# Order of the pairs in the first block of a merged projection stage: four plain pairs instead of three ahead of the first one with seven products

## The chip, the cores and the metric

One core of one Trainium2 chip runs the kernel. The metric is the device time of one execution in microseconds (us); less is better. The engines of the core are TensorE (PE, matrix multiplies), VectorE (DVE), ScalarE (ACT), GpSimd (POOL) and SyncE (SP, which here only issues loads). They run side by side and wait for one another through semaphores.

## The reference

A decoder layer of 256 positions and 2048 channels in float32. Latent attention and a gated short convolution run on the same normalised input. Each is projected back to 2048 channels, and the two are merged by gates that are projections of the input:

```python
proj = jnp.einsum('bsd,de->bse', h, w_in)          # ... z_mla, c_in, b_gate, c_gate, z_conv, g_mla, g_conv
...
y_mla = jnp.einsum('bse,ed->bsd', attn, w_o_mla)
...
y_conv = jnp.einsum('bse,ed->bsd', b_gate * conv * jax.nn.silu(z_conv), w_o_conv)
merged = jax.nn.sigmoid(g_mla) * y_mla + jax.nn.sigmoid(g_conv) * y_conv
out = jnp.einsum('bsd,de->bse', merged, w_out)
x = x + _rmsnorm(out, post_norm_g)
```

The merged stage, of which this document tells, computes the four projections of the line `merged = ...`: the two gates and the two outputs y_mla and y_conv, each 256 x 2048 by 2048 x 2048.

## The kernel before

**Precision.** Every float32 operand is split into a high part (a copy on ACT that rounds it, `whi`, `th`, `mix` hi) and a low part (the rest, a subtraction on DVE, `wlo`, `tl`, `mix` lo); `split_act` (L281) does both. A product (L264) is three matmuls: high by high, high by low, low by high. All matmuls are recorded at L90 and keep the order of the program on PE (L88).

**Weights.** All weights come in units of up to 128 x 2048 values (1 MB). `plan` lists them in the order of their use. `ahead` (L237) loads a unit into one of three `raw` tiles, up to three units ahead (SP issues the loads, in this order, L173), and splits the unit after the one that is now taken (`split_unit`, L180). A plain unit is split in two halves of 1024 columns, each into a `whi` and a `wlo` tile; there are five tiles of each, used in turn (L212, L213). So a high half is written only when PE is done with the half that held its tile before.

**The merged stage** has four projections n (0 and 1 the gates, 2 and 3 the outputs), and each has two blocks c of 1024 output columns. A block sums over eight pairs of 128 input channels. One unit of weights is one pair: four quarters of 512 columns (two channel groups by two column groups), and the two halves t of the 256 positions make a 2 x 2 by 2 x 2 block product. A plain pair takes its eight products (24 matmuls), into the banks p2, q3, q4 and d22. For the pairs in `fast` the kernel uses a scheme of seven products (21 matmuls, L1033 to L1039) instead, in the order p1, q5, q7, q6, p2, q3, q4, into seven banks. This is done in projections 0 and 1: pairs 0, 3 and 5 (`FAST`), except in the very first block, (0, 0), where only pairs 0 and 3 are (L144).

**What a pair with seven products needs.** On the side of the weights, `split_seven` (L218) makes three sums on DVE (`ts`, L224: one of 1024 columns and two of 512) and splits them too (`th` and `tl`; the names t1 to t4 are their quarters; two tiles of each). On the side of the input, `mixed(k)` (L1004) makes on DVE one sum (`xr`, L1008) and four differences (`xm`, L1012) of the input's blocks, and splits the result into `mix`. This is kept for all four blocks that use it, so `mixed` runs only in block (0, 0): `between` calls it for pair 0 at the block's place 1, for pair 3 at place 3 and for pair 5 at place 5 (L1106). `xr` and `xm` share two tiles (`ev`). These tiles lie where the stage before had its own, and can be written only when that stage's last steps on DVE are done.

**What comes after the seven products.** `first_sums` (L1052: one copy on ACT, L1053, and four sums on DVE) joins the banks p1, q5, q6 and q7 into the gate tiles. It is called at the place after the last pair with seven products (L1068). `last_sums` (L1059) adds p2, q3, q4 and d22 when the block is over, and a sigmoid follows on ACT (L1115). PSUM has eight banks, and a block uses all of them, so the next block may write a bank only when these sums have read it.

**What sets the order.** The matmuls keep program order, as do some helpers (`tc.keep_in_program_order`). The order of the other instructions on DVE and ACT is set when the kernel is built, by a planner that simulates the program and takes at each point the ready instruction that comes first in program order. On the chip each engine runs its list in that order.

The change touches `pair_order[0, 0]` (L142), which the plan of the loads (L148), and `fast_block` (L1025) follow.

Of the kernel before, what the change touches and what calls it, by code (L numbers as in the profile page):

```python
# [84 lines left out]
def tile_layer(ctx: ExitStack, tc: tile.TileContext, xw, w0, xb, x, pos, pvec, post_g, wc, wz, wcv, wkr, wqk, wqr, wv, cwr, wd, wo, out):  # L85
# [53 lines left out]
            u_head[i][j] = add(wcv[i, j])  # L139

    pair_order = {(n, c): list(range(PAIRS)) for n in range(4) for c in range(2)}
    pair_order[0, 0] = [1, 2, 4, 0, 6, 3, 5, 7]  # L142
    fast = {(n, c): FAST if n < 2 else () for n in range(4) for c in range(2)}
    fast[0, 0] = FAST[:2]  # L144
    u_d, seven = {}, set()
# [1201 lines left out]
```

## Time and profile before

| | |
|---|---|
| median of 3 runs | 1035.17 us |
| the three runs | 1033.79, 1035.17, 1035.41 us |
| the profiled execution | 1034.48 us |
| its span, first to last instruction | 1032.7 us |
| busy: PE, DVE, ACT, POOL | 1022.6, 747.4, 543.9, 179.0 us |
| mean granted clock of TensorE | 0.997 |
| the merged stage's first block, (0, 0) | 590.23 to 639.00 us of the span |

A row of the timeline has the start in us from the span's start, the duration, engine, line of the kernel, operation, output and inputs by the names of their tiles, the number of like instructions that were merged into the row, and in brackets the idle time of the engine before it with what ended that. Several banks show under a short name: p1 and p2 as `p`, q3 to q7 as `q`, d22 as `d`. A row of the waits says who waited for whom. Where the trace knows no releaser, it says "issue". A matmul starts 0.227 us after the one before it when nothing holds it, and its own 0.39 us overlaps the next.

### The profile page before, as it was taken

Reading aid. Unit: us, or ns where it says so; the run is one execution under the profiler, and the core shown is the slowest. Engines: PE = TensorE matmul, PEld = TensorE weight load, DVE = VectorE, ACT = ScalarE, POOL = GpSimd, SP = SyncE. Lnnn points to the kernel's source line nnn. Section 1 sums busy time; section 2 is a strip of 40 time slices with the busy share of each in tenths; the row PEclk is TensorE's granted clock in tenths of the full one; section 3 lists DMA queues with packets and bytes.
Section 4 is the critical chain, followed back from the end, with each engine's and each line's share of the span. In section 5 each row is a group of like instructions: output and inputs, shape, how many; then the busy total and the mean of one; then the engine's idle time right before and its main releaser. Section 6 shows DMA issues by size and latency. Waiting matters only on the chain.

```text
span 1032.7 us, 12827 instructions
## 1 busy us (share of the span) xinstructions
PE 1022.6 (99%) x4651; PEld 851.5 (82%) x4651; DVE 747.4 (72%) x1062; ACT 543.9 (53%) x764; POOL 179.0 (17%) x344
## 2 busy tenths in 40 slices
PE   9999999999999999999999989999999999999998
PEld 7888888888888888888888868888888888888886
DVE  7588777787777777777877798898875554756572
ACT  7665545655456454564555546555654443344451
POOL 4540421104301223112133120000000000214000
PEclk9999999999999999999999989999999999999999
DMA  9775866568665676757676755555555555577852
GB/s 357 276 260 202 279 205 234 213 201 282 218 246 197 220 263 211 273 192 244 229 269 222 260 183 178 226 206 204 204 198 182 193 202 196 197 258 246 344 184 81
DMA packets 44528, 233.26 MB, mean 226 GB/s; under 512 B 7953, under 2 KB 10513, under 8 KB 21553
## 3 DMA queue, kind: packets, MB, share of 16 engines
q1 hardware_dynamic: 32400, 199.67, 54.8%
q0 software_dynamic: 11632, 29.48, 8.8%
q10 hardware_dynamic: 432, 3.29, 0.8%
q8 instruction: 36, 0.59, 0.2%
q14 instruction: 28, 0.22, 0.1%
HBM read 215.66 MB, written 12.58 MB: 221 GB/s over the span
## 4 chain that ended last, share of the span: by engine, by line
PE 97%; DVE 2%; DMA 0%; ACT 0%; issue 0%
PE cv L90 34%; PE sq L90 17%; PE q L90 8%; PE z L90 8%; PE out L90 8%; PE p L90 4%; PE d L90 2%; PE kn L90 2%; PE qa L90 2%; PE qn L90 2%; PE vv L90 2%; PE ckv L90 2%; PE sc L90 1%; PE qr L90 1%; PE o L90 1%; DVE wlo L283 1%
## 5 line engine op out<-in xcount | busy, mean ns | idle before, releaser
L283 DVE TENSOR_TENSOR wlo<-raw,whi 128x1024 fp32r<-128x1024 f32 (+1 forms) x370 | 431.8, 1179 | 202.8 <-ACT whi L282 195.4
L282 ACT ACTIVATE whi<-raw 128x1024 fp32r<-128x1024 f32 (+1 forms) x372 | 373.2, 1021 | 376.0 <-PE cv L90 116.9
L90 PE MATMUL cv<-whi,x_both 128*128 128x512 f32 x1024 | 319.8, 389 | 0.0
L90 PEld LDWEIGHTS cv<-whi,x_both 128*128 128x128 f32 x1024 | 192.3, 188 | 39.4
L90 PE MATMUL cv<-wlo,x_both 128*128 128x512 f32 x512 | 199.6, 390 | 0.0
L90 PE MATMUL sq<-whi,x_both 128*128 128x512 f32 x384 | 118.8, 389 | 0.0
L90 PEld LDWEIGHTS cv<-wlo,x_both 128*128 128x128 f32 x512 | 96.1, 188 | 19.5 <-DVE wlo L283 0.2
L90 PEld LDWEIGHTS sq<-whi,x_both 128*128 128x128 f32 x384 | 72.1, 188 | 15.0
L90 PE MATMUL z<-whi,x_both 128*128 128x512 f32 x256 | 80.0, 389 | 0.0
L90 PE MATMUL out<-whi,x_both 128*128 128x512 f32 x256 | 79.0, 389 | 0.0
L90 PE MATMUL sq<-wlo,x_both 128*128 128x512 f32 x192 | 74.7, 389 | 0.0
L367 POOL DMA_DIRECT2D far<-g x32 | 17.4, 551 | 322.5 <-DVE g L1138 289.9
L367 POOL DMA_DIRECT2D far<-via x64 | 35.2, 556 | 179.2 <-DVE via L359 178.9
L90 PEld LDWEIGHTS out<-whi,x_both 128*128 128x128 f32 x256 | 48.1, 188 | 9.9
L90 PEld LDWEIGHTS z<-whi,x_both 128*128 128x128 f32 x256 | 48.1, 188 | 9.9
L90 PE MATMUL q<-whi,x_both 128*128 128x512 f32 x168 | 55.1, 389 | 0.0
L90 PE MATMUL z<-wlo,x_both 128*128 128x512 f32 x128 | 49.8, 389 | 0.0
L90 PE MATMUL out<-wlo,x_both 128*128 128x512 f32 x128 | 49.8, 389 | 0.0
L90 PE MATMUL p<-whi,x_both 128*128 128x512 f32 x128 | 46.6, 391 | 0.0
L90 PEld LDWEIGHTS sq<-wlo,x_both 128*128 128x128 f32 x192 | 36.0, 188 | 7.4
L367 POOL DMA_DIRECT2D far<-cw x48 | 26.1, 551 | 79.1 <-DVE cw L359 79.1
L90 PE MATMUL sq<-whi,cv_first 128*128 128x512 f32 x128 | 39.7, 389 | 0.0
(253 smaller groups left out, 1433.0 us busy)
## 6 DMA issues: line engine op xcount, KB each, us to landing
raw<-wcv_dram SPq DMA_DIRECT2D x64, 1024.0 KB, 5.9
raw<-wd_dram SPq DMA_DIRECT2D x64, 1024.0 KB, 4.8
raw<-wz_dram SPq DMA_DIRECT2D x16, 1024.0 KB, 4.8
raw<-wo_dram SPq DMA_DIRECT2D x16, 1024.0 KB, 5.0
raw<-wqk_dram SPq DMA_DIRECT2D x8, 1024.0 KB, 6.1
cw<-cwr_dram POOLq DMA_DIRECT2D x24, 256.0 KB, 6.2
raw<-wc_dram SPq DMA_DIRECT2D x4, 1024.0 KB, 10.4
raw<-wv_dram SPq DMA_DIRECT2D x4, 1024.0 KB, 4.8
```

The costliest lines, as they stand in the source:

```text
L90: return tc.keep_in_program_order(nc.tensor.matmul(*a, **kw))
L282: a = nc.scalar.activation(hi, src, AF.Copy)
L283: b = nc.vector.tensor_tensor(lo, src, hi.bitcast(F32), op=ALU.subtract)
L367: tc.keep_in_program_order(queue.dma_start(out=f[i], in_=m))
```

## The change

One line. In block (0, 0) pair 6 is taken before pair 0 instead of after it, and pair 5 before pair 3. Pairs 0 and 3 are the ones with seven products. The places at which `mixed` is called stay as they are. `first_sums` follows the last pair with seven products, so it moves from place 6 to place 7, with one plain pair (7) behind it instead of two (5 and 7).

```diff
     pair_order = {(n, c): list(range(PAIRS)) for n in range(4) for c in range(2)}
-    pair_order[0, 0] = [1, 2, 4, 0, 6, 3, 5, 7]
+    pair_order[0, 0] = [1, 2, 4, 6, 0, 5, 3, 7]
     fast = {(n, c): FAST if n < 2 else () for n in range(4) for c in range(2)}
     fast[0, 0] = FAST[:2]
```

The loads, the splits and the products of these units follow the new order, since all three go by the plan. The matmuls, sums and splits are the same in number and size, and every bank sums the same terms, in another order.

## The prediction

> **What bounds the kernel now.** I read the waits of TensorE (PE) first, over the whole execution: who was waited for, the us in total, how often, and the longest.
>
> ```profile
> PE q L90 <- issue: 2.3, 1, 2.3
> PE q L90 <- DVE mix L283: 1.4, 1, 1.4
> PE idle L90 <- PEq L1335: 0.8, 1, 0.8
> PE qa L90 <- ACT whi L282: 0.5, 1, 0.5
> PE fin L90 <- ACT dg L1223: 0.4, 1, 0.4
> ```
>
> PE is the bound, and it waits five times in all. The last three are the program's head and tail. The first two have "q" as their output, the products of the merged stage, and they belong together. The timeline of PE shows where (start, duration, line, operation, idle before it and what ended that):
>
> ```profile
> 606.59 0.39 PE L90 MATMUL p<-whi,x_both 128*128 128x512 f32 x1
> 606.82 0.39 PE L90 MATMUL p<-wlo,x_both 128*128 128x512 f32 x1
> 607.04 0.39 PE L90 MATMUL p<-whi,x_both 128*128 128x512 f32 x1
> 609.74 0.77 PE L90 MATMUL q<-th,mix 128*128 128x512 f32 x1 [2.31 <-issue]
> 610.30 0.63 PE L90 MATMUL q<-tl,mix 128*128 128x512 f32 x1
> 612.31 1.22 PE L90 MATMUL q<-th,mix 128*128 128x512 f32 x2 [1.38 <-DVE mix L283]
> ```
>
> This is pair 0, the first pair with seven products: p1 (three matmuls), then q5, the first product with a mixed operand. It stands still at once, and again two matmuls later. How long should it take? The view by stretch gives its length, the busy us of PE, its weight loads, VectorE (DVE), ScalarE (ACT) and GpSimd, the granted clock, the DMA share and GB/s. First pair 0, then the plain pair 6 and the seven-product pair 3 behind it, cut at each pair's first matmul:
>
> ```profile
> 606.59:617.92 11.33, 7.64 (x23) 5.34 (x21) 10.78 (x18) 5.75 (x8) 0.00 (x0) 0.70 0.56 208
> 617.92:623.36 5.44, 5.44 (x26) 4.50 (x24) 3.90 (x7) 2.65 (x4) 0.00 (x0) 1.00 0.55 193
> 623.36:628.12 4.76, 4.76 (x23) 3.94 (x21) 4.76 (x6) 4.18 (x6) 0.00 (x0) 1.00 0.30 79
> ```
>
> Undisturbed, a plain pair takes 5.44 us (24 matmuls, 0.227 each) and a seven-product pair 4.76 (21). Pair 0 took 11.33: **6.57 us lost**. The idle time explains 3.69 of it (2.31 + 1.38); the other 2.88 is the clock, which is 0.70 in this stretch. In stretches of 5 us, from 605:
>
> ```profile
> 605.00:610.00 5.00, 2.69 (x12) 1.98 (x11) 5.00 (x7) 3.47 (x4) 0.25 (x1) 0.95 0.79 265
> 610.00:615.00 5.00, 3.62 (x8) 2.37 (x8) 4.93 (x10) 0.53 (x1) 0.00 (x0) 0.50 0.62 259
> 615.00:620.00 5.00, 5.00 (x21) 4.04 (x20) 4.52 (x10) 3.69 (x5) 0.00 (x0) 0.87 0.13 16
> ```
>
> Read as half speed, a mean of 0.95 is 0.5 us slow in the first stretch, all of the second is, and 1.3 us of the third: the clock fell near 609.5, some 2.1 us after PE fell idle (607.04 + 0.23 + a little), and came back near 616.3. So here a wait of about 2 us costs its length and then 2.9 us more; a shorter one, as an estimate from these rows, its length alone.
>
> The Trainium skill ("TensorE: Matmul & The Clock Gate", What's actually happening) puts the fall to half speed after an idle window of about 3.4 us. The trace disagrees, since a single gap of 2.31 us was followed by it; by that page of the skill the two waits would have cost 3.69 us alone, and removing them would give 1034.71 - 3.69 = 1031.0. It gets no chance of its own below, as the 6.57 us are measured.
>
> The same rows tell what PE waited for: DVE is busy 5.00 of 5.00 and 4.93 of 5.00, ACT far less. The timelines of DVE and of ACT:
>
> ```profile
> 599.83 0.66 DVE L1008 TENSOR_TENSOR xr<-x_both 128x512 f32<-128x512 f32 x1
> ...
> 606.42 1.23 DVE L224 TENSOR_TENSOR ts<-raw 128x1024 f32<-128x1024 f32 x1
> 607.55 1.23 DVE L283 TENSOR_TENSOR wlo<-raw,whi 128x1024 fp32r<-128x1024 f32 x1
> 608.69 0.69 DVE L1008 TENSOR_TENSOR xr<-x_both 128x512 f32<-128x512 f32 x1
> 609.29 1.23 DVE L283 TENSOR_TENSOR wlo<-raw,whi 128x1024 fp32r<-128x1024 f32 x1
> 610.42 1.23 DVE L283 TENSOR_TENSOR tl<-ts,th 128x1024 fp32r<-128x1024 f32 x1
> 611.56 0.69 DVE L283 TENSOR_TENSOR mix<-xm,mix 128x512 fp32r<-128x512 f32 x1
> 612.16 0.69 DVE L224 TENSOR_TENSOR ts<-ts,raw 128x512 f32<-128x512 f32 x1
> ```
>
> ```profile
> 606.17 2.00 ACT L282 ACTIVATE whi<-raw 128x1024 fp32r<-128x1024 f32 x2 [2.81 <-PE d L90]
> 608.08 1.04 ACT L282 ACTIVATE th<-ts 128x1024 fp32r<-128x1024 f32 x1
> 609.03 0.61 ACT L282 ACTIVATE mix<-xm 128x512 fp32r<-128x512 f32 x1
> ```
>
> mixed(0) begins at 599.83 and its low part ends at 612.25, with DVE never idle between. The "issue" of 2.31 us ends when ACT's mix ends (609.03 + 0.61 = 609.64), the 1.38 us when DVE's mix ends. Nothing was slow: 12.4 us of DVE work stood between the start and the end of pair 0's preparation, and only 7.4 us of PE work. Counting the halves of each unit (ring of five tiles per high and low part, so each high half waits until a former pair gives its tile back) the rows of DVE belong to: pair 3's sum (606.42), pair 6's second half (607.55), mixed(3) (608.69), pair 3's first half (609.29), pair 0's t2/t4 (610.42), its mix (611.56).
>
> **The change part by part.** No instruction is added or removed: the same weights, matmuls, splits and sums. Pair 6 changes places with pair 0, and pair 5 with pair 3; four things move.
>
> *PE's arrival.* Pair 6 now takes 606.59 to 612.03, and pair 0 starts then. q5 needs the high mix and t1 at 612.03 + 3 x 0.227 = 612.71, and the low mix, its third matmul, at 613.16.
>
> *The mix's readiness.* DVE's start at 599.83 does not move: the pairs before it are the same. Between there and 612.25 pair 6's two halves stand as before, one of them earlier in place of pair 0's first half: a swap at no cost. Pair 3's sum and first half (1.13 each, start to start) give way to the first half of pair 5, which is plain and has no sums: minus 1.13, so the low mix ends near 611.1. At the other end, the schedule might still put pair 3's three sums in front (1.13 + 0.6 + 0.6, the latter the spacing of rows as wide): 613.4. The two ends are 2.0 us before the need and 0.3 after it; I take the first, because mixed(0) and pair 0's split come before pair 3's in program order. Pair 5's second half can't get ahead cheaply: its tile comes free when PE is done with pair 6, near 611.6. If DVE were to wait for it, with 1.0 of ACT, 1.13 of DVE and the mix's 0.69, the mix would end near 614.5, 1.3 us late. The high mix ends near 609.6 as now, 3 us early.
>
> So the stall's 6.57 us go, or all but 0.3 to 1.3 of them.
>
> *What is late next: pairs 5, 3 and 7.* They start at 616.79, 622.23 and 626.99. For pair 3, t1/t3 may be written only after q7 of pair 0 has read theirs (near 614.2), t2/t4 after its q4 (616.8). By the DVE and ACT rows (1.04 and 1.13 each) they are ready near 616 and 620, where 622.9 and 624.3 is needed: no cost, some 4 us of cover. SP's queue issues the loads in the new order of units, three tiles deep; pair 0's comes one place later and pair 6's one sooner. Size and median us from issue to landing:
>
> ```profile
> raw<-wd_dram SPq DMA_DIRECT2D x64, 1024.0 KB, 4.8
> ```
>
> A load takes 4.8 us and a plain unit 5.44 of PE, with three tiles ahead: nothing.
>
> *first_sums, one unit later.* It now runs with one plain pair behind the last seven-product pair instead of two. That is the new risk, as block (0,1) opens with a seven-product pair that needs the same banks at once. In the trace:
>
> ```profile
> 623.34 1.23 DVE L224 TENSOR_TENSOR ts<-raw 128x1024 f32<-128x1024 f32 x1 [1.54 <-DMA raw<-wd_dram]
> ...
> 627.96 0.69 DVE L1050 TENSOR_TENSOR ev<-q,ev 128x512 f32<-128x512 f32 x1
> ...
> 634.29 0.69 DVE L1050 TENSOR_TENSOR g<-q,g 128x512 f32<-128x512 f32 x1
> ...
> 636.62 0.69 DVE L1050 TENSOR_TENSOR g<-p,ev 128x512 f32<-128x512 f32 x1
> ...
> 641.53 1.22 DVE L283 TENSOR_TENSOR wlo<-raw,whi 128x1024 fp32r<-128x1024 f32 x1
> ```
>
> The first of its four DVE instructions is at 627.96; the fourth, which frees q5's bank, starts at 634.29 and ends at 634.98: 8.7 us after q6 of pair 3 ended (623.36 + 12 x 0.227 + a drain = 626.3). The block ends at 639.00 (628.12 + 2 x 5.44) and the next q5 is due 0.68 later, so 4.7 us were to spare. After the change, q6 ends at 625.2, the block at 632.43, and the next q5 is due at 633.11: 7.9 us. With the old spacing q5's bank is 0.8 us late. With its four instructions back to back (0.69 each) it would be 5 us early. Between these stands DVE's load: the work from 612.2 to 634.98 is the same but for 1.1 us done earlier and 1.2 of pair 3's sums moved back, and the idle 1.54 us (a load that waited for the split of pair 3) can be filled, as that tile is now freed by pair 5's split some 4 us sooner. DVE then ends that list near 633.4 (634.98 - 1.54). That is 0.3 us late; I take **0.3 us**, below the length that moved the clock.
>
> Sum against the profiled execution: 1034.48 - 6.57 + 0.3 = 1028.2. The three runs and the profiled one average 1034.71, with the median 0.46 above that; I put the forecast at 1034.71 - 6.27 = **1028.4**. All that follows in the program is PE work without a wait until the tail, so the gain carries through.
>
> **The rivals.**
> 1. *The wait moves to the bank of q5.* DVE is busy throughout, so its backlog may delay the start of first_sums: begun near 628 instead of 625.2 and spaced as in the trace (7.0 us from 627.96 to 634.98), the bank comes at 635.0, 1.9 us late. If the clock holds, the gain is 4.7 (1030.0); if it falls, another 2.9 goes and 1.8 is left (1032.9). For it: the old spacing alone overruns. Against it: DVE has 1.54 us of idle to win back. Chance 0.15, nearly all of it still over 0.2% (2.1 us) faster; 0.2% is about what a measurement of this kernel can tell from no change.
> 2. *The wait stays with pair 0.* The whole order of DVE's queue is made anew from the program, and could put as much in front of the mix as PE has gained, 5.44 us; with today's lateness that gives today's loss, 1034.7. Against it: so much ready work is not there before 613. Chance 0.09.
> 3. *Slower.* The place is again the start of block (0,1), but the last of first_sums is queued behind both low halves of pair 1 of that block. In the trace the second of these ended 3.7 us after its block's start (the row at 641.53), since its high half waits for the last plain pair's tile. Then q5 waits until 632.43 + 3.7 + 0.6 = 636.7, 3.6 us, the clock falls (2.9), and last_sums, 2.3 us further on in the trace (636.62 after 634.29), hold p2 as well: 8.8 lost against 6.57 won, 1036.9. It decides from a bank that is free later than about 637. Against it: first_sums stand ahead of that split in program order. Chance 0.06.
>
> That the change does not do what it says is excluded: matmuls keep program order, and the loads follow the plan's order.
>
> **How the numbers follow.** Forecast 0.70 (1027 to 1030), bank 0.15, unchanged 0.09, slower 0.06. Faster: 0.70 and nearly all of 0.15, so 0.84; same 0.10; slower 0.06. The range: below, the fastest run less the whole loss, 1033.79 - 6.57 = 1027.2, with 0.2 for scatter: 1027.0. Above, it takes in most of the bank rival with the fallen clock: 1032.6. About 0.17 lies outside.
>
> **What would show it.** Right: no idle of PE before the first q<-th,mix; pair 0 takes 4.76 us with clock 1.00 from 612.03; the low mix ends before 613; the block ends near 632.4; DVE's idle 1.54 before the ts of block (0,1) is gone; q5 of that block follows p1 within 0.5 us. Wrong: a wait "<-DVE mix" that stays; or a new one "<-DVE g L1050" at the start of block (0,1), as long as the one that went.

## The result, and the profile after

| | before | after |
|---|---|---|
| median of 4 runs each | 1034.48 us (1033.61 to 1035.41) | 1039.99 us (1039.29 to 1040.51) |
| ratio | | 1.0053 (95%: 1.0035 to 1.007) |
| span of the profiled execution | 1032.7 us | 1038.1 us |

The changed kernel is 0.5% slower. The forecast was 1028.4 us, 0.6% faster. The two longest waits of PE, over the whole execution after the change (the other three, at the head and the tail, are 1.4 us together):

```profile
PE q L90 <- DVE g L1050: 6.9, 1, 6.9
PE p L90 <- ACT ev L1053: 1.5, 1, 1.5
```

The two waits at pair 0's mix (2.3 and 1.4 us) are gone, and two others stand in their place, together more than twice as long. The timeline of PE at the place of the old wait, then at that of the new ones:

```profile
612.39 0.39 PE L90 MATMUL p<-whi,x_both 128*128 128x512 f32 x1
612.62 0.39 PE L90 MATMUL q<-th,mix 128*128 128x512 f32 x1
```

```profile
632.36 0.39 PE L90 MATMUL d<-whi,x_both 128*128 128x512 f32 x1
634.28 0.50 PE L90 MATMUL p<-whi,x_both 128*128 128x512 f32 x1 [1.53 <-ACT ev L1053]
634.62 0.40 PE L90 MATMUL p<-wlo,x_both 128*128 128x512 f32 x1
634.86 0.40 PE L90 MATMUL p<-whi,x_both 128*128 128x512 f32 x1
642.20 0.80 PE L90 MATMUL q<-th,mix 128*128 128x512 f32 x1 [6.95 <-DVE g L1050]
...
649.19 0.39 PE L90 MATMUL p<-whi,x_both 128*128 128x512 f32 x1
```

q5 of pair 0 now follows p1 at the undisturbed distance. The new waits are at the first matmuls of block (0, 1): p1 waits for p1's bank, which the copy of first_sums (L1053) reads, and q5 for q5's bank, which its last sum (L1050) reads. Block (0, 1) was due at 632.36 + 0.23 = 632.59 and its pair 0 takes 4.76 us, so pair 1 was due at 637.35. It came at 649.19 (the row after the dots): **11.84 us lost**, 8.48 of it waits and 3.36 the clock. Less the old 6.57, that is 5.3 us, and the spans differ by 5.4.

By stretch (length, busy PE, weight loads, DVE, ACT, GpSimd, clock, DMA share, GB/s), cut at the pairs from pair 0 on, and then over the wait:

```profile
611.92:616.68 4.76, 4.76 (x22) 3.94 (x21) 4.64 (x8) 3.75 (x5) 0.00 (x0) 1.00 0.47 160
616.68:622.12 5.44, 5.44 (x25) 4.50 (x24) 5.44 (x8) 2.58 (x4) 0.00 (x0) 1.00 0.70 261
622.12:626.88 4.76, 4.76 (x21) 3.67 (x20) 4.76 (x9) 3.50 (x5) 0.00 (x0) 1.00 0.35 96
626.88:632.32 5.44, 5.44 (x25) 4.50 (x25) 4.74 (x7) 1.95 (x3) 0.00 (x0) 1.00 0.69 268
632.32:640.00 7.68, 1.41 (x5) 0.49 (x4) 6.74 (x9) 3.58 (x5) 0.00 (x0) 0.86 0.49 179
640.00:650.00 10.00, 7.80 (x22) 6.26 (x23) 5.78 (x8) 5.32 (x7) 0.00 (x0) 0.59 0.00 0
```

The first four rows are block (0, 0) without a gap. What is first_sums waiting for? The timeline of DVE in the changed kernel, rows from mixed(5)'s sum (`xr`) to first_sums' own (`ev`, `g`; the `mix` at 622.65 is still mixed(3)'s):

```profile
622.05 0.68 DVE L1008 TENSOR_TENSOR xr<-x_both 128x512 f32<-128x512 f32 x1
622.65 0.68 DVE L283 TENSOR_TENSOR mix<-xm,mix 128x512 fp32r<-128x512 f32 x1
...
626.12 0.48 DVE L1012 TENSOR_TENSOR xm<-xr 128x128 f32<-128x128 f32 x2
...
631.34 0.28 DVE L1012 TENSOR_TENSOR xm<-xr,xm 128x128 f32<-128x128 f32 x1
633.26 1.23 DVE L283 TENSOR_TENSOR wlo<-raw,whi 128x1024 fp32r<-128x1024 f32 x1 [1.64 <-ACT whi L282]
...
635.54 0.68 DVE L283 TENSOR_TENSOR mix<-xm,mix 128x512 fp32r<-128x512 f32 x1
...
638.47 0.68 DVE L1050 TENSOR_TENSOR ev<-q,ev 128x512 f32<-128x512 f32 x1
...
640.87 2.00 DVE L1050 TENSOR_TENSOR g<-q,g 128x512 f32<-128x512 f32 x3
```

And of ACT:

```profile
632.17 1.06 ACT L282 ACTIVATE whi<-raw 128x1024 fp32r<-128x1024 f32 x1 [3.49 <-PE d L90]
633.13 0.61 ACT L282 ACTIVATE mix<-xm 128x512 fp32r<-128x512 f32 x1
633.65 0.58 ACT L1053 ACTIVATE ev<-p 128x512 f32<-128x512 f32 x1
```

mixed(5) ends at 636.22 instead of 621.8, 14 us later, and first_sums begins only behind its last difference, although p1's bank had been ready since 623 and q6's since 625.3. Both write the two `ev` tiles. The copy (`ev`, 633.65) is behind mixed(5)'s last difference (631.34) and the first sum (638.47) behind its low mix (635.54). On ACT, mixed(5)'s high mix also stands behind a high half (632.17) that had waited for PE's last plain pair, and the copy behind both: the 2.0 us from the last difference's end (631.62) to the copy go by in ACT's list.

So the theory to test, **A: the tiles**: first_sums can't begin before mixed(5) has given back the `ev` tiles, and in the changed order mixed(5) is late. Its rival, **B: the load**: one plain pair (5.44 us) behind the last seven-product pair is too short for DVE's work, whatever tiles it uses.

### The profile page after: what moved, and what is told of

Its sections match the earlier page's. It is cut to its first block, busy times and chain, and to the rows that moved or that the text cites. A ratio compares the mean times of both kernels' runs of the same rounds, so it can differ in the third digit from the quotient of the medians.

```text
span 1038.1 us, 12825 instructions
## 1 busy us (share of the span) xinstructions
PE 1023.6 (99%) x4651; PEld 852.3 (82%) x4651; DVE 747.0 (72%) x1062; ACT 544.5 (52%) x764; POOL 180.3 (17%) x344
## 4 chain that ended last, share of the span: by engine, by line
PE 98%; DVE 1%; DMA 0%; ACT 0%; issue 0%; ACTq 0%
PE cv L90 34%; PE sq L90 17%; PE q L90 9%; PE z L90 8%; PE out L90 8%; PE p L90 4%; PE d L90 3%; PE qa L90 2%; PE kn L90 2%; PE qn L90 2%; PE vv L90 2%; PE ckv L90 2%; PE sc L90 1%; PE qr L90 1%; PE o L90 1%; PE kr L90 0%
```

## Experiments

**First sums with tiles of their own.** In the changed kernel:

```diff
-        t_a, t_b = (evens(f"ev{i}_{n}{c}")[:, :] for i in range(2))
+        if n == c == 0:
+            t_a, t_b = (gate[1][0][:, i * R : (i + 1) * R] for i in range(2))
+        else:
+            t_a, t_b = (evens(f"ev{i}_{n}{c}")[:, :] for i in range(2))
```

> The changed order, but in block (0, 0) the two tiles that first_sums writes (t_a, t_b) lie in the gate tile of projection 1, which is idle then, instead of in the two ev tiles that mixed also uses. Theory A (shared tiles): the new wait at the start of block (0, 1) is there because t_a and t_b can't be written before mixed(5) has given its two tiles back; so with tiles of their own the waits of 1.5 and 6.9 us fall to under 1 us together, the low clock with them, and the time is 1028 +- 1.5 us. Theory B (load of VectorE): one plain pair behind the last seven-product pair is too short for VectorE's work whatever tiles it uses; q5's bank stays at least 3 us late and the time is 1034 to 1038.

Measured: 1031.81 us, ratio to before 0.9973 (0.9962 to 0.9984). Its longest waits of PE:

```profile
PE q L90 <- ACT mix L282: 1.9, 1, 1.9
PE q L90 <- DVE g L1053: 0.9, 1, 0.9
```

The 8.5 us of waits in block (0, 1) fell to 2.8, the clock stayed at 1.00 there, and the time fell by 8 us against the changed kernel, below that of before. Most of the loss is A. It isn't all: 2.8 us is more than the "under 1 us" that A expected, and the time lies between the ranges of A (to 1029.5) and of B (from 1034). Its DVE timeline, from the first sum to mixed(5)'s low mix:

```profile
628.16 0.68 DVE L1053 TENSOR_TENSOR g<-q,g 128x512 f32<-128x512 f32 x1
...
634.96 1.28 DVE L1053 TENSOR_TENSOR g<-q,g 128x512 f32<-128x512 f32 x2
...
639.56 0.68 DVE L283 TENSOR_TENSOR mix<-xm,mix 128x512 fp32r<-128x512 f32 x1
```

first_sums now begins 10 us earlier and is done before mixed(5), which ends later still. The wait row names `mix`, but the mix that ACT ended just before q5 starts (636.35, against 636.39) is mixed(5)'s, which q5 of pair 0 doesn't read. What q5 needs is the sum that frees its bank, the second of the two in the row at 634.96; it ends at 636.24. The wait of 0.9 us is at another bank, q4's, which last_sums frees. DVE is busy without a gap before both, as B has it; whether these 2.8 us are its load is not shown by this run. Another 0.8 us of waits came in the attention stage, with this kernel's new schedule, and are no part of the question.

**mixed(5) one block later.** The tiles stay shared; the other party to the sharing is moved, in the changed kernel:

```diff
-                if n == c == 0 and i in (1, 3, 5):
+                if n == c == 0 and i in (1, 3):
                     mixed(FAST[i // 2])
+                if n == 0 and c == 1 and i == 1:
+                    mixed(5)
```

> The changed order, with mixed(5) called at place 1 of block (0, 1) instead of place 5 of block (0, 0); pair 5 has seven products only from block (0, 1) on. Theory A (shared tiles): first_sums finds its tiles free, no wait over 1 us at the start of block (0, 1), 1028 +- 1.5 us. Theory B (load of VectorE): 2.4 us of VectorE work leave the block, so the 8.5 us of waits shrink to about 6 and the time is 1036 +- 1.5.

Measured: 1030.24 us, ratio 0.996 (0.9947 to 0.9972); the clock is 1.00 throughout.

```profile
PE q L90 <- DVE g L1050: 1.8, 2, 0.9
```

A second way of taking the conflict away has the same outcome: two waits of 0.9 us are left of 8.5 (again one at q5's bank and one at q4's), where B expected 6. The time is 9.7 us below that of the changed kernel, and 0.7 us above the range of A.

**The two halves of the change.** Order 1, 2, 4, 6, 0, 3, 5, 7:

```diff
-    pair_order[0, 0] = [1, 2, 4, 6, 0, 5, 3, 7]
+    pair_order[0, 0] = [1, 2, 4, 6, 0, 3, 5, 7]
```

> Half of the change: order 1, 2, 4, 6, 0, 3, 5, 7. Pair 0 comes later, but first_sums keeps its place with two plain pairs behind it. Both theories: no wait at pair 0 and none at the start of block (0, 1), since first_sums has 10.9 us; pair 3 follows pair 0 at once, its t2/t4 can be written only when pair 0 is done and come 1 to 3 us late. 1028 to 1033 us. A wait at block (0, 1) as long as now would speak against both.

Measured: 1035.08 us, ratio 1.0003 (0.9994 to 1.0012), above the range expected.

```profile
PE q L90 <- ACT mix L282: 2.6, 1, 2.6
PE q L90 <- DVE mix L283: 1.6, 1, 1.6
```

No wait at pair 0 and none at block (0, 1), as expected, but waits at pair 3 that are a little longer than the old ones (4.2 us against 3.7). It is not the t2/t4 that were named: it is mixed(3), whose differences come behind mixed(0)'s low mix. With nothing between pairs 0 and 3, the wait for a mix has only moved from the one to the other.

The other half, order 1, 2, 4, 0, 6, 5, 3, 7:

```diff
-    pair_order[0, 0] = [1, 2, 4, 6, 0, 5, 3, 7]
+    pair_order[0, 0] = [1, 2, 4, 0, 6, 5, 3, 7]
```

> The other half: order 1, 2, 4, 0, 6, 5, 3, 7. The old wait at pair 0 stays (6.6 us with the clock). Theory A (shared tiles): with PE 6.6 us later, mixed(5) is done in time and first_sums has its tiles, so no wait at block (0, 1): 1034.5 +- 1.5 us, as before the change. Theory B (load of VectorE): first_sums has again one plain pair only, a wait of 3 us or more at block (0, 1) comes on top: 1038 to 1046.

Measured: 1034.29 us, ratio 0.9995 (0.9986 to 1.0004): as before the change, as A said.

```profile
PE q L90 <- issue: 2.3, 1, 2.3
PE q L90 <- DVE mix L283: 1.6, 1, 1.6
```

This kernel too has one plain pair behind the last seven-product pair, and no wait at block (0, 1). PE stands still at pair 0, and in that time DVE gets mixed(5) done (low mix at 621.66, against 635.54 in the changed kernel). So the late place of first_sums does no harm by itself. This run doesn't say more against B, since the stall gave DVE time in hand as well as free tiles: it stands idle for 1.43 us before 623.77 and for 1.76 us before 629.70. What sets the tiles apart from the load are the first two experiments.

**Controls in the order of before.** The tiles of the first experiment, and the move of the second, each applied to the kernel before (the same edits as above):

> Control: the order of before, with the tiles of first_sums in the idle gate tile as in the first experiment. Theory A (shared tiles): in the order of before mixed(5) is done at 621.8, before first_sums begins, so the sharing costs nothing there and nothing moves: the wait at pair 0 stays, 1034.5 +- 1.5 us. If the tiles by themselves were worth something whatever the order, it would be 1032 or less.

> Control for the second experiment: the order of before, with mixed(5) at place 1 of block (0, 1). Theory A (shared tiles): the wait at pair 0 is older than mixed(5) and stays with its low clock, and first_sums had its tiles in time anyway, so 1034.5 +- 1.5 us. If it is 1032 or less, the move of mixed(5) brings something by itself and the second experiment's gain isn't the changed order's.

Measured: 1034.17 us, ratio 0.9999 (0.999 to 1.0008), and 1034.74 us, ratio 1.0005 (0.9996 to 1.0014). Neither does anything alone. The gain of the first two experiments needs both: the new order, and the tiles out of the way.

**Tiles of their own for mixed(3) and mixed(5).** In the changed kernel:

```diff
-        tmp = evens(f"xr{k}")
-        f = tmp[:, :].rearrange("p (j s) -> p j s", j=2)
+        o = 2 * R * (FAST.index(k) - 1)
+        tmp = gate[1][0][:, o : o + R] if k else evens(f"xr{k}")[:, :]
+        f = tmp.rearrange("p (j s) -> p j s", j=2)
...
-        raw = evens(f"xm{k}")
+        raw = gate[1][0][:, o + R : o + 2 * R] if k else evens(f"xm{k}")
```

> The changed order, with the tiles of mixed(3) and mixed(5) in the idle gate tile; mixed(0) and first_sums have the ev tiles. Theory A: first_sums finds its tiles free, no wait over 2 us at the start of block (0, 1). But nothing holds mixed(3) and mixed(5) back any more, so their sums run ahead of pair 0's low mix on VectorE: some 3 us of work, and pair 0 waits 2 to 3 us where it waits nothing now. 1030 to 1034 us. Theory B (load of VectorE): the load is the same, so the bank of q5 stays several us late: 1036 to 1039.

Measured: 1033.02 us, ratio 0.9984 (0.9975 to 0.9992).

```profile
PE q L90 <- DVE mix L283: 1.9, 1, 1.9
PE q L90 <- issue: 1.4, 1, 1.4
```

No wait is left at block (0, 1). In its place pair 0 waits again, 3.2 us, since its low mix now ends at 617.6 instead of 612.5: the sums and differences of the other two `mixed` run ahead of it (mixed(0)'s last difference starts at 611.73 instead of 606.66, and its splits come behind other halves). The shared tiles had a use: they held back work that was not due yet.

**The same tiles in the order 1, 2, 4, 6, 0, 3, 5, 7:**

> The order 1, 2, 4, 6, 0, 3, 5, 7 of the third experiment, with the tiles of mixed(3) and mixed(5) in the idle gate tile. Theory A also for pair 3's wait in the third experiment (the differences of mixed(3) can't be written before mixed(0) has given its tile back): the waits at pair 3 (2.6 and 1.6 us) go, 2 to 3 us of wait come at pair 0 as in the sixth experiment, none over 1 us at block (0, 1): 1029 to 1033 us. If pair 3 waits because VectorE is short of time between two adjacent seven-product pairs, its waits stay and the time is 1034 or more.

Measured: 1036.21 us, ratio 1.0019 (1.001 to 1.0028), above the range expected.

```profile
PE q L90 <- DVE mix L283: 1.7, 1, 1.7
PE q L90 <- DVE tl L283: 1.6, 1, 1.6
PE q L90 <- issue: 1.0, 1, 1.0
```

Pair 3's wait for its mix is gone, as the theory of the tiles has it, and 2.7 us came at pair 0. But pair 3 waits all the same, 1.6 us, now for the low part of its t2/t4 (`tl`). So two adjacent seven-product pairs wait with or without the tiles, as the rival said. That DVE is short of time there, its reason, is not shown: DVE stands idle for 1.33 us before 621.66. The high part of t2/t4 (ACT, 622.76) came only when pair 0 was done (pair 3 starts at 622.38), which the third experiment had expected, and on DVE a sum of 1024 columns (624.03) stood before the low part.

**What is left: load or order?** The second experiment, with the sum and the differences of mixed(3) and mixed(5) on GpSimd:

```diff
+        eng = nc.gpsimd if k else nc.vector
-        nc.vector.tensor_tensor(f, x_both[:, ks, :S].bitcast(F32), x_both[:, ks, S:].bitcast(F32), op=ALU.add)
+        eng.tensor_tensor(f, x_both[:, ks, :S].bitcast(F32), x_both[:, ks, S:].bitcast(F32), op=ALU.add)
...
-        minus = lambda o, a, b: nc.vector.tensor_tensor(o, a, b, op=ALU.subtract)
+        minus = lambda o, a, b: eng.tensor_tensor(o, a, b, op=ALU.subtract)
```

> The second experiment (mixed(5) at place 1 of block (0, 1)), with the sum and the four differences of mixed(3) and mixed(5) on GpSimd instead of VectorE. It asks what the waits of 0.9 and 0.9 us are that were left in the second experiment. If they are VectorE's load (about 2 us less of it before these points), they fall under 0.3 us each and the time is 1028.5 +- 1 us. If they are the planner's spacing of the chain of first_sums, they stay: 1030.2 +- 1.

Measured: 1029.62 us, ratio 0.9951 (0.9939 to 0.9964), the lowest of all; like the second experiment it beats both kernels clearly. One wait is left, 1.6 us at q5; the second, at q4's bank, is gone.

```profile
631.69 1.72 DVE L283 TENSOR_TENSOR tl<-ts,th 128x1024 fp32r<-128x1024 f32 x1
633.33 1.28 DVE L1051 TENSOR_TENSOR g<-q,g 128x512 f32<-128x512 f32 x2
```

The sum that frees q5's bank is not earlier (it ends at 634.61, against 634.23 in the second experiment). While GpSimd was at mixed(5) (630.2 to 636.1), a DVE subtraction of 1024 columns took 1.72 us instead of 1.22. So this doesn't tell load and order apart at q5: the relieved DVE was slowed in the same stretch. That stays open.

## Why the prediction was wrong

**Right: the first half.** Pair 0 began at 611.94 (forecast 612.03), its low mix ended at 612.49 (forecast between 611.1 and 613.4), q5 came without a wait and the clock stayed at 1.00. Pairs 5, 3 and 7 had no wait that the list shows, and the block ended at 632.59 (forecast 632.43). The old 6.57 us were won. One reading in it was wrong without cost: the "4 us of cover" of pair 3 counts only the weight sums. Its own low mix ended at 623.33, and the matmul that reads it, due at 623.27, started at 623.39. mixed(3) too had been strung out by the splits.

**Wrong: the step "first_sums, one unit later".** It took DVE's old list from 612.2 to 634.98, corrected it by about 1 us each way, and put the last of first_sums at 633.4, 0.3 us late. It ended near 642.15, and the waits cost 11.84 us instead of 0.3. The prediction's own sign of being wrong, a new wait "<-DVE g L1050" at the start of block (0, 1), is the one that came. Two things were wrong in the step.

- It looked at what first_sums reads, the banks, and at DVE's load. It didn't look at what first_sums writes. Its two tiles are those of `mixed`, so the start of first_sums hangs on the end of mixed(5). The kernel's own lines had that (`evens` at L1005, L1009 and L1048). The first two experiments show that this is the cause: with the tie cut, in either way, 5.7 to 6.7 of the 8.5 us of waits go, and the low clock with them.
- It took the spacing of the old rows as given. In the trace of before mixed(5) was done at 621.8, but that was a gift of the stall: PE stood, few tiles came free, and DVE had little else that was ready. The order with only pair 5 ahead of pair 3 shows it: with the stall kept and first_sums just as late, mixed(5) ends at 622.3 and nothing is lost. With PE running on, splits fill every place between the linked steps of mixed(3) and mixed(5).

**The rivals.** The third, "slower", had the place (the start of block (0, 1)), the kind of wait (q5's bank) and the size within 3 us (8.8 us lost forecast, 11.84 measured; 1036.9 us against 1039.99), but another mechanism, and p1's bank, which the runs showed to be late too, was not in it. It was given a chance of 0.06, with the argument that first_sums stand ahead of that split in program order. The queue that it named did form: the first of the four sums (638.47) stands behind both low halves of pair 1 (629.07 and 633.26). But it is no cause of its own, as with own tiles the sums that free the banks are ahead of the second half again (634.96 against 636.16); held back by the tiles, they had lost their place. The first rival, a bank of q5 that is late without any tie, is close to what is left when the tie is cut: 1.9 us forecast, 1.9 measured with own tiles and 0.9 with mixed(5) moved. Whether DVE's load is the reason stays open, as said. So its time (1030.0) and the forecast's (1028.4) stand close to the 1030.2 and 1029.6 us of the kernels that have the new order without the conflict.

**The clock.** The estimate that a wait shorter than some 2 us costs its length alone held for single waits: 1.9 us (own tiles) and 1.6 us (GpSimd) left it at 1.00. It did not hold for two in a row: where mixed(3) and mixed(5) have their own tiles, in the changed order, two waits of 1.4 and 1.9 us with 0.7 us of work between them lowered it. The stretches of 3 us there, from 612:

```profile
612.00:615.00 3.00, 1.69 (x8) 1.07 (x6) 3.00 (x6) 2.57 (x4) 0.00 (x0) 1.00 0.73 300
615.00:618.00 3.00, 1.08 (x3) 0.69 (x4) 3.00 (x4) 0.99 (x2) 0.00 (x0) 0.72 0.38 79
618.00:621.00 3.00, 3.00 (x8) 2.33 (x8) 2.09 (x5) 1.06 (x1) 0.00 (x0) 0.50 0.64 270
621.00:624.00 3.00, 3.00 (x10) 2.35 (x10) 2.93 (x3) 1.18 (x2) 0.00 (x0) 0.65 0.00 0
```

The clock is at 1.00 in the first stretch, which holds most of the first wait, and falls in the second, in which PE was busy for 1.08 of 3 us. The Trainium skill ("TensorE: Matmul & The Clock Gate", What's actually happening) has the gate watch how busy PE was of late, over windows of about 3.4 us. These rows agree with the watching, as two waits count together that do nothing singly. They do not show the length of the window, and in the kernel before the clock fell within one wait of 2.31 us.

## What to carry to other kernels

Before a step is called "only later", list what it writes as well as what it reads, and for each shared buffer who has it before; a buffer that was free in the old trace may have been free because of the very stall that goes. When a stall is removed, the work that ran in its shade must find another place: reread every chain of small linked steps as if the queue between them were full. And a wait moves more often than it goes: each of the seven kernels here that put pair 6 ahead of pair 0 had new waits, from 1.6 to 8.5 us together.

## What the runs showed of the hardware

GpSimd and DVE at the same time: the five steps of mixed(5) that take 1.7 us on DVE (0.68, 0.48, 0.28 and 0.28 in the changed kernel's rows) took 5.7 us on GpSimd. Six DVE subtractions of 1024 columns ran in part beside GpSimd's steps of mixed(3) and mixed(5) in that kernel; they took 1.48 to 2.00 us, against 1.22. The kernel was still 0.6 us faster than the second experiment, with ranges of the runs that don't overlap (1028.99 to 1029.71, and 1030.2 to 1031.33). That is not shown to be GpSimd's gain: in the two traces the merged stage begins 0.3 us apart (590.08 and 590.39), before any step that was moved, and the waits in it differ by 0.2 us.
